# A hybrid decoder layer on one core: gate products in pairs of passes by width, and weight parts in pieces of 1024 columns

## The chip, the cores and the metric

The kernel runs on one core of one Trainium2 chip. The metric is the device time of one execution in microseconds (us), as the median of several runs. The engines of the core run side by side, each through its own queue in order: PE multiplies matrices (TensorE), ACT (ScalarE) and DVE (VectorE) do the elementwise work, POOL (GpSimd) a few additions, and SP (SyncE) issues the transfers from memory. They wait for each other on semaphores.

## The reference

One decoder layer, 256 tokens of 1024 features, in float32: a gated feed-forward network, three token mixers (A: sliding window attention, B: block attention, M: attention into 256 memory tokens) whose results are weighted by gates, and a second gated network, each followed by a layer norm.

```python
x = layer_norm(DN_ALPHA * x + 0.5 * swiglu(x, ffn1_w_gate, ffn1_w_up, ffn1_w_down), ln1_g, ln1_b)
h = x @ w_in + b_in
q_a, k_a, v_a, q_b, k_b, v_b, q_m, gates = jnp.split(h, offsets, axis=-1)
y_a = sliding_window_gqa(q_a, k_a, v_a, attn_sinks) @ w_proj_swa
y_b = moba_attention(q_b, k_b, v_b) @ w_proj_moba
y_m = memory_cross_attention(q_m, mem, w_mem_kv, b_mem_kv) @ w_proj_mem
g = jax.nn.sigmoid(gates.reshape(B, S, N_BRANCH, D))
mixed = (g[:, :, 0] * y_a + g[:, :, 1] * y_b + g[:, :, 2] * y_m) @ w_out
x = layer_norm(DN_ALPHA * x + mixed, ln2_g, ln2_b)
x = layer_norm(DN_ALPHA * x + 0.5 * swiglu(x, ffn2_w_gate, ffn2_w_up, ffn2_w_down), ln3_g, ln3_b)
```

## The kernel before

**Numbers in two parts.** Float32 values are held as a high and a low part, `hi` and `lo`, and a product is the sum of three: hi*hi, hi*lo and lo*hi. `split` (lines 129 to 132) makes the parts: ACT casts the source into `hi` (line 131), then DVE subtracts `hi` from the source and writes `lo` (line 132).

**Weights.** All weights come in chunks of 128x2048 elements, 1 MB each, in the order of `plan`. SP loads a chunk into one of three `raw` buffers (line 153), and `part_to` splits it into one of four pairs `whi`, `wlo`, so a `raw` is free for the next load once DVE has written its last `wlo`. `part_to` splits a chunk whole, 2048 columns at a time, or in four pieces of 512 columns (line 169): in pieces for the first six chunks, and for the 42 chunks from the last four of the first network's down projection to the gate and up weights of the second network's chunk 3, so for all that lies between the two networks' gate and up products. A chunk is prepared two chunks ahead of its use.

**Products.** One output tile is 128 features by 256 tokens in one of eight PSUM buffers `ps`. `feature_tile` (line 199) makes it with `product`: for each of 8 blocks of 128 inputs three matmuls of 256 columns, lines 187 to 189, 24 in all, summed in place. `feature_tile_2` (line 203) makes the same tile in two passes: 8 matmuls of 512 columns (line 209), in which `whi` meets high and low part of the tokens side by side, and 8 of 256 columns (line 211) for `wlo`. Its two halves have to be added: `added` (line 213) copies one half out with ACT (line 216) into `b`, and DVE adds the other half to it (line 217). The networks use `feature_tile_2`.

**The gates.** There are 24 gate tiles, named (c, b, j): column group c of 0 to 3, mixer b of 0 to 2, half j of 0 or 1. `gate_chunk` makes the two tiles of a (c, b). For c = 0 and 1 they stand among the attention's steps: `feature_tile`, then one ACT instruction, tanh with bias, from `ps` to `gates` (line 611). For c = 2 and 3 they stand among the mixing steps and already use `feature_tile_2`, `added`, and a tanh from `gates` to `gates` (lines 613 to 615).

**The attention.** `scores` (line 514) multiplies queries and keys (line 528, PE), on DVE adds the distance term (line 535, A and B) and takes row maxima (540, or 532 for M), negates them (543), lets ACT take the exponentials (551), and on DVE inverts the sums (560) and scales the probabilities (563). `turn` (line 566) transposes one pair of heads on PE (line 575) and splits the result into `p` (a 512 wide piece and, for A and B, a 256 wide one); `weigh` (line 582) multiplies `p` with the values `vab` (lines 187 to 189: two matmuls with the high part of `p`, one with the low part, on line 188) and splits the outcome into `qk_a` or `qk_b`. Lines 617 to 652 set the order in which all of this is written: `scores("b")`, gates (0, 1), `scores("m")`, gates (0, 2), `turn("b", 0)`, gates (1, 0), `weigh("b", 0)`, and so on.

**Who sets the order.** SP's queue stands as written. For PE, ACT and DVE a scheduler sets the order when the kernel is built, out of what is written and its own view of what is ready, so a change of sizes or of instructions shifts the others as well.

Of the kernel before, what the change touches and what calls it, by code (L numbers as in the profile page):

```python
# [13 lines left out]
AF = mybir.ActivationFunctionType  # L14
# [3 lines left out]
P = 128  # L18
S = 256
# [96 lines left out]
def hybrid_layer(ctx: ExitStack, tc: tile.TileContext, a: dict, out: bass.AP):  # L116
    nc = tc.nc
# [11 lines left out]
    def split(src, hi, lo):  # L129

        nc.scalar.copy(hi, src)  # L131
        return nc.vector.tensor_sub(lo, src, hi.bitcast(F32))  # L132
# [9 lines left out]
    index = {key: i for i, (key, _, _) in enumerate(chunks)}  # L142
# [4 lines left out]
    def load_to(n):  # L147
        while done["raw"] <= min(n, len(chunks) - 1):
            i = done["raw"]
            raw_of[i] = raws.tile([P, 2048], F32, name="raw")  # L150
            n_ = 512 if i < 4 else 2048
            for o in range(0, 2048, n_):
                nc.sync.dma_start(out=raw_of[i][:, o : o + n_], in_=a["w"][i][:, o : o + n_])
            done["raw"] += 1

    def part_to(n):
        while done["part"] <= min(n, len(chunks) - 1):
            i = done["part"]
            load_to(i)
            raw, how = raw_of.pop(i), chunks[i][1]  # L160
            if how:
                t = "1" if how == "leadg" else "2"
                hi = acts.tile([P, 2048], F32R, name="lhi", tag="A" + t)
                lo = acts.tile([P, 2048], F32R, name="llo", tag="B" + t)
            else:
                hi = parts.tile([P, 2048], F32R, name="whi")
                lo = parts.tile([P, 2048], F32R, name="wlo")

            n_ = 512 if i < 6 or index["mk"] - 4 <= i <= index["u", 2, 3] else 2048
            lows[i] = [split(raw[:, o : o + n_], hi[:, o : o + n_], lo[:, o : o + n_]) for o in range(0, 2048, n_)]  # L170
            part_of[i] = (hi, lo)
            done["part"] += 1

    def weights(key, ahead=2):
        i = index[key]
        load_to(i + 6)
        part_to(i + ahead)
        return part_of.pop(i)

    def prepare(key):  # L180
        part_to(index[key])

    def product(ps, terms, first=True, last=True):

        n = len(terms)
        for i, ((lh, ll), (rh, rl)) in enumerate(terms):
            nc.tensor.matmul(ps, lh, rh, start=first and i == 0, stop=False)  # L187
            nc.tensor.matmul(ps, lh, rl, start=False, stop=False)  # L188
            nc.tensor.matmul(ps, ll, rh, start=False, stop=last and i == n - 1)  # L189

    def two(t, *s):
        return tuple(x[s] for x in t)
# [6 lines left out]
    def feature_tile(ps, w, col, x, n=KD):  # L199

        product(ps, [(two(w, ALL, slice(k * 256 + col, k * 256 + col + P)), two(x, ALL, k, ALL)) for k in range(n)])

    def feature_tile_2(ps, w, col, x, ks=range(KD), parts_=(0, 1)):

        for part in parts_:
            for k in ks:
                wk = w[part][:, k * 256 + col : k * 256 + col + P]
                if part == 0:
                    nc.tensor.matmul(ps, wk, x.both[:, k], start=k == 0, stop=False)  # L209
                else:  # L210
                    nc.tensor.matmul(ps[:, S:], wk, x[0][:, k], start=False, stop=k == KD - 1)  # L211

    def added(dst, ps):

        b = work.tile([P, 512], F32, name="b", tag="w")[:, :S]
        nc.scalar.copy(b, ps[:, S:])  # L216
        nc.vector.tensor_add(dst, ps[:, :S], b)
# [23 lines left out]
    def tokens_of(name):  # L241

        both = acts.tile([P, KD, 2, S], F32R, name=name, tag="xT")
        return Parts(both)
# [39 lines left out]
    bcol = const.tile([P, NB], F32, name="bcol")  # L284
# [158 lines left out]
    x1T = tokens_of("x1T")  # L443
# [18 lines left out]
    for j in range(2):  # L462
        ps = mm.tile([P, 512], F32, name="ps")
# [4 lines left out]
    for t in range(2):  # L468
        ps = mm.tile([P, 512], F32, name="ps")
# [130 lines left out]
    gate_w = {}  # L600

    def gate_chunk(c, b, js=(0, 1)):
        if js[0] == 0:
            gate_w[c, b] = weights(("gt", c, b))
        for j in js:
            ps = mm.tile([P, 512], F32, name="ps")
            k = 12 + 8 * b + 2 * c + j
            g = gates[:, c % 2, 2 * b + j, :]
            if c < 2:
                feature_tile(ps[:, :S], gate_w[c, b], j * P, x1T)  # L610
                nc.scalar.activation(g, ps[:, :S], AF.Tanh, bias=bcol[:, k : k + 1], scale=0.5)  # L611
            else:
                feature_tile_2(ps, gate_w[c, b], j * P, x1T)
                added(g, ps)
                nc.scalar.activation(g, g, AF.Tanh, bias=bcol[:, k : k + 1], scale=0.5)

    tiles("qa0", [(0, qa, 0), (1, qa, 1)])
    tiles("qa1", [(2, qa, 2), (3, ka, 0)])
# [11 lines left out]
    weigh("a", 1)  # L630
    turn("a", 2)
    gate_chunk(0, 0)
    weigh("a", 2)
    scores("b")
    gate_chunk(0, 1)
    scores("m")
    gate_chunk(0, 2)
    turn("b", 0)
    gate_chunk(1, 0)
# [115 lines left out]
```

## Time and profile before

| | us |
|---|---|
| median of 3 runs (580.15 to 580.31) | 580.24 |
| the profiled execution | 580.73 |
| span of the profiled execution, first to last instruction | 578.9 |
| PE busy | 568.6 |
| DVE busy | 397.6 |
| ACT busy | 309.5 |
| POOL busy | 23.6 |

PE is shown busy in 98% of the span, but its matmuls overlap and the end of one is modelled, so for PE the distance from start to start is what counts. ACT and DVE are busy in 53% and 69% of the span, unevenly: in the attention, between 240 and 300 us, both are near full. A row of a timeline gives the start from the span's begin, the length, the engine, the line and what is written from what; "x4" merges four that follow each other, and a bracket names idle time of the engine before the row and what ended it.

### The profile page before, as it was taken

The numbers are of one execution on the slowest core, as the hardware profiler recorded it, in microseconds if no ns is written. First come the engines' busy times: TensorE is split into PE (matmuls) and PEld (weight loads), VectorE is DVE, ScalarE is ACT, GpSimd is POOL, SyncE is SP. The second block draws the span as 40 slices with busy tenths as digits, with TensorE's granted clock in tenths as the row PEclk, the third lists the DMA queues.
The fourth block names the chain that finished last, engine by engine and source line by source line (L and its number), as shares of the span: only waits on it lengthen the run. The fifth ranks groups of instructions, "written<-read, shape, count | busy, mean of one in ns | idle before, by whom it ended". The sixth has DMA issues, their size and how long they took to land.

```text
span 578.9 us, 8791 instructions
## 1 busy us (share of the span) xinstructions
PE 568.6 (98%) x3470; PEld 505.9 (87%) x3470; DVE 397.6 (69%) x609; ACT 309.5 (53%) x543; POOL 23.6 (4%) x37
## 2 busy tenths in 40 slices
PE   8999999999999999999999999999999999999994
PEld 7888888888888998999999989888888888888884
DVE  5887667764446977698787677996667657654336
ACT  6884556644333653964975665643565554633300
POOL 2000000000000000000002022210000000000001
PEclk9999999999999999999999999999999999999998
DMA  8887647745553474084163554536554555545201
GB/s 272 309 301 289 239 170 282 267 157 212 197 174 142 146 278 158 3 341 167 29 232 110 215 188 175 218 145 254 192 208 166 198 190 177 216 151 213 74 1 72
DMA packets 18025, 108.98 MB, mean 188 GB/s; under 512 B 2112, under 2 KB 2368, under 8 KB 5696
## 3 DMA queue, kind: packets, MB, share of 16 engines
q1 hardware_dynamic: 17984, 108.43, 52.0%
q8 instruction: 27, 0.44, 0.3%
q14 instruction: 14, 0.11, 0.1%
HBM read 107.37 MB, written 1.05 MB: 187 GB/s over the span
## 4 chain that ended last, share of the span: by engine, by line
PE 93%; ACT 3%; DVE 2%; DMA 1%; issue 0%; POOLq 0%; SPq 0%; DVEq 0%
PE ps L209 29%; PE ps L187 15%; PE ps L188 15%; PE ps L189 15%; PE ps L211 15%; ACT whi L131 1%; ACT sc_b L551 1%; DMA raw<-in_w_dram 1%; PE ps L575 1%; PE ps L255 1%; DVE sc_b L535 0%; DVE m L540 0%; PE ps L528 0%; ACT gates L611 0%; DVE r L419 0%
## 5 line engine op out<-in xcount | busy, mean ns | idle before, releaser
L132 DVE TENSOR_TENSOR wlo<-raw,whi 128x512 fp32r<-128x512 f32 (+2 forms) x234 | 233.8, 1030 | 127.0 <-ACT whi L131 122.6
L131 ACT CAST whi<-raw 128x512 fp32r<-128x512 f32 (+2 forms) x234 | 196.6, 882 | 121.7 <-PE ps L189 59.7
L209 PE MATMUL ps<-x0T,whi 128*128 128x512 f32 x352 | 89.5, 393 | 1.0 <-ACT whi L131 1.0
L209 PEld LDWEIGHTS ps<-x0T,whi 128*128 128x128 f32 x352 | 62.9, 189 | 12.3 <-ACT whi L131 1.4
L188 PE MATMUL ps<-wlo,hh 128*128 128x512 f32 (+1 forms) x198 | 72.5, 366 | 0.0
L187 PE MATMUL ps<-whi,hh 128*128 128x512 f32 (+1 forms) x198 | 72.5, 366 | 0.0
L189 PE MATMUL ps<-whi,hl 128*128 128x512 f32 (+1 forms) x198 | 72.3, 365 | 0.0
L209 PE MATMUL ps<-x2T,whi 128*128 128x512 f32 x288 | 72.2, 392 | 0.0
L209 PEld LDWEIGHTS ps<-x2T,whi 128*128 128x128 f32 x288 | 51.8, 189 | 9.3
L187 PE MATMUL ps<-x1T,whi 128*128 128x256 f32 x192 | 55.2, 287 | 0.3 <-ACT sc_m L551 0.3
L216 ACT COPY b<-ps 128x256 f32<-128x256 f32 x92 | 33.6, 368 | 39.6 <-PE ps L211 38.2
L188 PE MATMUL ps<-x1T,whi 128*128 128x256 f32 x192 | 54.3, 283 | 0.0
L189 PE MATMUL ps<-x1T,wlo 128*128 128x256 f32 x192 | 54.3, 283 | 0.0
L211 PEld LDWEIGHTS ps<-x0T,wlo 128*128 128x128 f32 x352 | 48.7, 190 | 4.2 <-DVE wlo L132 0.3
L211 PE MATMUL ps<-x0T,wlo 128*128 128x256 f32 x352 | 50.0, 282 | 0.0
L187 PEld LDWEIGHTS ps<-whi,hh 128*128 128x128 f32 x198 | 37.3, 188 | 6.1
L189 PEld LDWEIGHTS ps<-whi,hl 128*128 128x128 f32 x198 | 37.2, 188 | 6.2
L188 PEld LDWEIGHTS ps<-wlo,hh 128*128 128x128 f32 x198 | 37.3, 188 | 6.0
L211 PEld LDWEIGHTS ps<-x2T,wlo 128*128 128x128 f32 x288 | 39.3, 190 | 2.8
L211 PE MATMUL ps<-x2T,wlo 128*128 128x256 f32 x288 | 40.2, 282 | 0.0
L187 PEld LDWEIGHTS ps<-x1T,whi 128*128 128x128 f32 x192 | 36.8, 191 | 0.8 <-ACT sc_m L551 0.5
L188 PEld LDWEIGHTS ps<-x1T,whi 128*128 128x128 f32 x192 | 36.8, 192 | 0.0
(173 smaller groups left out, 762.8 us busy)
## 6 DMA issues: line engine op xcount, KB each, us to landing
raw<-in_w_dram SPq DMA_DIRECT2D x92, 1024.0 KB, 4.8
raw<-in_w_dram SPq DMA_DIRECT2D x16, 256.0 KB, 5.4
ln<-in_ln_dram SPq DMA_DIRECT2D x3, 1024.0 KB, 6.9
xT<-in_xT_dram SPq DMA_DIRECT2D x4, 256.0 KB, 6.5
x_sb<-in_x_dram SPq DMA_DIRECT2D x1, 1024.0 KB, 8.4
raw<-in_memT_dram SPq DMA_DIRECT2D x1, 1024.0 KB, 4.8
out_dram<-r SPq DMA_DIRECT2D x3, 256.0 KB, 2.1
brow<-in_by_column_dram SPq DMA_DIRECT2D x1, 387.0 KB, 8.5
```

The lines of the kernel that those rows point to most:

```text
L131: nc.scalar.copy(hi, src)
L132: return nc.vector.tensor_sub(lo, src, hi.bitcast(F32))
L187: nc.tensor.matmul(ps, lh, rh, start=first and i == 0, stop=False)
L188: nc.tensor.matmul(ps, lh, rl, start=False, stop=False)
L189: nc.tensor.matmul(ps, ll, rh, start=False, stop=last and i == n - 1)
L209: nc.tensor.matmul(ps, wk, x.both[:, k], start=k == 0, stop=False)
L211: nc.tensor.matmul(ps[:, S:], wk, x[0][:, k], start=False, stop=k == KD - 1)
L216: nc.scalar.copy(b, ps[:, S:])
L255: nc.tensor.transpose(ps[:, j * P : (j + 1) * P], src[:, k * P : (k + 1) * P], ident)
L551: nc.scalar.activation(sc[:, e, c0:c1], raw[e][:, c0:c1], AF.Exp, bias=negm[:, e, t : t + 1], scale=SCALE, accum_out=ssum[:, e, t : t + 1])
L575: nc.tensor.transpose(pt[:, s * n + j * P : s * n + (j + 1) * P], sc[:, 2 * i + s, c : c + P], ident)
```

## The change

For c = 0 and 1 the gate tiles are now made as those of c = 2 and 3 are: two passes of 16 matmuls instead of 24 matmuls, a copy on ACT, an addition on DVE, and the tanh from `gates` to `gates`. And where the weights' parts were made in pieces of 512 columns between the two networks' gate and up products, the pieces are now 1024 columns; the first six chunks keep theirs.

```diff
-            n_ = 512 if i < 6 or index["mk"] - 4 <= i <= index["u", 2, 3] else 2048
+            n_ = 512 if i < 6 else 1024 if index["mk"] - 4 <= i <= index["u", 2, 3] else 2048
...
-            if c < 2:
-                feature_tile(ps[:, :S], gate_w[c, b], j * P, x1T)
-                nc.scalar.activation(g, ps[:, :S], AF.Tanh, bias=bcol[:, k : k + 1], scale=0.5)
-            else:
-                feature_tile_2(ps, gate_w[c, b], j * P, x1T)
-                added(g, ps)
-                nc.scalar.activation(g, g, AF.Tanh, bias=bcol[:, k : k + 1], scale=0.5)
+            feature_tile_2(ps, gate_w[c, b], j * P, x1T)
+            added(g, ps)
+            nc.scalar.activation(g, g, AF.Tanh, bias=bcol[:, k : k + 1], scale=0.5)
```

With it the scheduler sets another order on ACT and DVE; on PE and SP the steps keep their places. Three places follow, first before, then after. Buffers carry a number that differs between the two programs.

ACT ahead of the exponentials of mixer B, from the last cast of `p` for A's second pair of heads: the two tiles of gates (0, 0), the result of A's third pair (`qk_a`), and the first tile of gates (0, 1). Before:

```order
L131 CAST p_2595<-ps_2592 128x256
L131 CAST qk_a_1949<-ps_2572 64x256
L131 CAST whi_2757<-raw_2331 128x512
L611 ACTIVATE gates_1951<-ps_2611,bcol_185 128x256
L131 CAST whi_2876<-raw_2413 128x512
L611 ACTIVATE gates_1951<-ps_2637,bcol_185 128x256
L131 CAST whi_2876<-raw_2413 128x512
L131 CAST qk_a_1949<-ps_2663 64x256
L131 CAST whi_2876<-raw_2413 128x512 x2
```

After:

```order
L131 CAST p_2531<-ps_2528 128x256
L216 COPY b_2560<-ps_2543 128x256
L611 ACTIVATE gates_1923<-gates_1923,bcol_185 128x256
L131 CAST whi_2784<-raw_2357 128x1024
L216 COPY b_2581<-ps_2564 128x256
L131 CAST whi_2784<-raw_2357 128x1024
L131 CAST qk_a_1921<-ps_2585 64x256
L611 ACTIVATE gates_1923<-gates_1923,bcol_185 128x256
L131 CAST qk_a_1921<-ps_2585 64x256
```

The tanh, which read `ps`, now reads what DVE's addition writes, and a cast of weights that stood apart from it stands behind it.

DVE at the same place, from the low part of that `p` to the first distance term of B. Before:

```order
L132 TENSOR_TENSOR p_2596<-ps_2592,p_2595 128x256
L132 TENSOR_TENSOR wlo_2758<-raw_2331,whi_2757 128x512 x2
L132 TENSOR_TENSOR wlo_2877<-raw_2413,whi_2876 128x512 x2
L132 TENSOR_TENSOR qk_a_1949<-ps_2663,qk_a_1949 64x256
L132 TENSOR_TENSOR wlo_2877<-raw_2413,whi_2876 128x512
L132 TENSOR_TENSOR qk_a_1949<-ps_2663,qk_a_1949 64x256
L535 SCALAR_TENSOR_TENSOR sc_b_2674<-dist_b_188,ps_2676 128x384
```

After:

```order
L132 TENSOR_TENSOR p_2532<-ps_2528,p_2531 128x256
L217 TENSOR_TENSOR gates_1923<-ps_2543,b_2560 128x256
L132 TENSOR_TENSOR wlo_2785<-raw_2357,whi_2784 128x1024
L217 TENSOR_TENSOR gates_1923<-ps_2564,b_2581 128x256
L132 TENSOR_TENSOR qk_a_1921<-ps_2585,qk_a_1921 64x256
L132 TENSOR_TENSOR wlo_2785<-raw_2357,whi_2784 128x1024
L132 TENSOR_TENSOR qk_a_1921<-ps_2585,qk_a_1921 64x256
L535 SCALAR_TENSOR_TENSOR sc_b_2596<-dist_b_188,ps_2598 128x384
```

The first addition stands behind the low part of `p`, and the `wlo` that follows it needs the `whi` that ACT casts behind the tanh of that addition.

DVE after the last scaling of M, from the low parts of `p` for B's first pair of heads to those of its second pair. Before:

```order
L132 TENSOR_TENSOR p<-ps,p 128x512
L132 TENSOR_TENSOR wlo<-raw,whi 128x512
L132 TENSOR_TENSOR p<-ps,p 128x256
L132 TENSOR_TENSOR wlo<-raw,whi 128x512 x5
L132 TENSOR_TENSOR qk_b<-ps,qk_b 64x256
```

After:

```order
L217 TENSOR_TENSOR gates<-ps,b 128x256 x2
L132 TENSOR_TENSOR p<-ps,p 128x512
L132 TENSOR_TENSOR wlo<-raw,whi 128x1024
L132 TENSOR_TENSOR p<-ps,p 128x256
L132 TENSOR_TENSOR wlo<-raw,whi 128x1024
L217 TENSOR_TENSOR gates<-ps,b 128x256
L132 TENSOR_TENSOR wlo<-raw,whi 128x1024
L217 TENSOR_TENSOR gates<-ps,b 128x256
L132 TENSOR_TENSOR wlo<-raw,whi 128x1024
L132 TENSOR_TENSOR qk_b<-ps,qk_b 64x256
```

Two additions stand ahead of the first `p`, and between the two pairs' `p` stand three pieces of 1024 and two additions instead of five pieces of 512; in both programs a `p` 128x512 follows the row of `qk_b`.

## Rows read from the trace of the kernel before

**Rows 1.** The chain of work that ended last, share of the span by engine.

```profile
PE 93%; ACT 3%; DVE 2%; DMA 1%; issue 0%; POOLq 0%; SPq 0%; DVEq 0%
```

**Rows 2.** Windows: stretch, its length, busy us and count of each engine, granted clock, DMA.

```profile
270.00:280.00 10.00, 9.70 (x90) 9.20 (x89) 6.99 (x20) 8.19 (x34) 0.00 (x0) 1.00 0.12 48
280.00:290.00 10.00, 10.00 (x82) 9.70 (x81) 9.24 (x23) 9.97 (x28) 0.00 (x0) 1.00 0.20 62
```

**Rows 3.** PE, timeline: first matmul of gates (0, 0), and the first of `weigh`.

```profile
255.78 0.36 PE L187 MATMUL ps<-x1T,whi 128*128 128x256 f32 x1
...
261.62 0.40 PE L187 MATMUL ps<-p,vab 128*128 128x512 f32 x1
```

**Rows 4.** The chain in order of time (start, length): one gate tile of c = 2.

```profile
312.46 1.84 PE ps L209 x8
314.30 0.95 PE ps L211 x8
```

**Rows 5.** Groups by line and shape: line, engine, count, busy us, mean ns, idle before.

```profile
L131 ACT CAST whi<-raw 128x512 fp32r<-128x512 f32 x182 | 103.5, 621 | 60.3 <-PE ps L189 29.9 <-DMA raw<-in_w_dram 12.2 <-PE ps L188 9.2
L131 ACT CAST whi<-raw 128x2048 fp32r<-128x2048 f32 x48 | 91.6, 1908 | 59.7 <-PE ps L189 29.8 <-PE ps L209 28.0 <-DMA raw<-in_w_dram 1.8
L216 ACT COPY b<-ps 128x256 f32<-128x256 f32 x92 | 33.6, 368 | 39.6 <-PE ps L211 38.2 <-issue 1.3
L615 ACT ACTIVATE gates<-gates,bcol 128x256 f32<-128x256 f32 x12 | 6.1, 509 | 4.3 <-DVE gates L217 4.3
L132 DVE TENSOR_TENSOR wlo<-raw,whi 128x512 fp32r<-128x512 f32 x182 | 122.2, 711 | 38.6 <-ACT whi L131 34.2 <-PE ps L211 4.0
L132 DVE TENSOR_TENSOR wlo<-raw,whi 128x2048 fp32r<-128x2048 f32 x48 | 110.1, 2293 | 86.6 <-ACT whi L131 86.6
L217 DVE TENSOR_TENSOR gates<-ps,b 128x256 f32<-128x256 f32 x12 | 5.0, 420 | 0.8 <-ACT b L216 0.6
```

**Rows 6.** DVE, timeline from A's `p` to B's scaling.

```profile
245.57 1.05 DVE L132 TENSOR_TENSOR p<-ps,p 128x512 fp32r<-128x512 f32 x2
...
260.20 0.42 DVE L132 TENSOR_TENSOR p<-ps,p 128x256 fp32r<-128x256 f32 x1
...
262.40 0.69 DVE L132 TENSOR_TENSOR wlo<-raw,whi 128x512 fp32r<-128x512 f32 x1 [0.57 <-ACT whi L131]
...
265.44 1.02 DVE L535 SCALAR_TENSOR_TENSOR sc_b<-dist_b,ps 128x384 f32<-128x384 f32 x2
...
277.48 2.84 DVE L563 TENSOR_SCALAR sc_b<-sc_b,rs 128x128 f32<-128x128 f32 x12
280.24 1.29 DVE L132 TENSOR_TENSOR wlo<-raw,whi 128x512 fp32r<-128x512 f32 x2
```

**Rows 7.** ACT, timeline: weights' casts ahead of M's exponentials, and the first of these.

```profile
277.45 1.13 ACT L131 CAST whi<-raw 128x512 fp32r<-128x512 f32 x2
278.48 0.47 ACT L551 ACTIVATE sc_m<-ps,negm 128x256 f32<-128x256 f32 x1
```

**Rows 8.** DVE, timeline: `p` of B's first and second pair of heads.

```profile
285.79 0.42 DVE L132 TENSOR_TENSOR p<-ps,p 128x256 fp32r<-128x256 f32 x1
...
289.47 0.67 DVE L132 TENSOR_TENSOR p<-ps,p 128x512 fp32r<-128x512 f32 x1
```

**Rows 9.** PE, timeline: the steps that take what DVE and ACT give.

```profile
247.52 0.28 PE L188 MATMUL ps<-p,vab 128*128 128x256 f32 x1
...
278.43 0.82 PE L575 MATMUL ps<-ident,sc_b 128*128 128x128 f32 x6
279.55 0.38 PE L187 MATMUL ps<-x1T,whi 128*128 128x256 f32 x1 [0.30 <-ACT sc_m L551]
...
286.27 0.38 PE L188 MATMUL ps<-p,vab 128*128 128x256 f32 x1
...
290.36 0.40 PE L188 MATMUL ps<-p,vab 128*128 128x512 f32 x1
...
291.19 0.39 PE L188 MATMUL ps<-p,vab 128*128 128x256 f32 x1
```

## The prediction

> **What bounds the kernel now.** I read the chain of waits first: 93% of what ended last is PE [rows 1], so the time is the sum of PE's start-to-start distances, and an edit counts only by what it does to that sum. Then the windows, to see where PE can be made to wait: in the attention DVE and ACT, idle a third to a half of the whole span, are busy 7 to 10 of 10 us [rows 2]. Then the timelines of the three engines there. In this stretch PE takes its operands almost the moment they are made. The transposes of B's probabilities start at 278.43, when the third of twelve scalings, begun at 277.48 and 0.24 apart, is just done [rows 6, 9]; the fourth, which the fourth transpose needs, leaves about 0.2. The matmul with B's first low part of `p` starts at 286.27, 0.06 after DVE's write of it that begins at 285.79 and lasts 0.42 [rows 8, 9]; that of the second pair at 290.36, after a write that ends at 290.14. One wait shows: 0.30 ahead of gates (1, 0), for a PSUM buffer that M's exponentials hold [rows 9]. The granted clock is full here (1.00) [rows 2]. So this stretch has next to no slack, and the change adds work to DVE and ACT in it.
>
> **What PE saves.** Two gate tiles by `feature_tile` stand from 255.78 to 261.62, 5.84 us [rows 3]. By two passes a tile is 1.84 + 0.95 = 2.79 [rows 4], two are 5.58, and with 0.1 for the slow first matmul after transposes (255.78 shows 0.36 in place of 0.28) 5.68. That is 0.16 for a pair, 0.08 a tile, and for the 12 tiles 0.95 us. No other PE instruction changes. This term is safe: from 0.9 to 1.1.
>
> **What ACT and DVE pay.** Each of the 12 tiles gains a copy on ACT (0.37) and an addition on DVE (0.42), and its tanh is one of 0.51 [rows 5]. Two that follow each other on an engine overlap by some 0.08 on DVE and 0.1 on ACT: two `wlo` of 512 take 1.29, not 1.42, two `whi` 1.13, not 1.24 [rows 6, 7, 5]. So the step is 0.33 for an addition and 0.27 for a copy, 4.0 us on DVE and 3.2 on ACT in sum. A piece of 1024 is read off between 512 and 2048: DVE 711 + (2293 - 711)/3 = 1240 ns, ACT 621 + (1908 - 621)/3 = 1050 ns [rows 5], against 1.29 and 1.13 for two of 512; so DVE wins about 0.06 and ACT about 0.08 for each of 84 pairs, 5 and 7 us over a third of the program. Where the engine waits anyway, outside the attention, neither sum touches PE. In the attention what counts is who stands in front of whom.
>
> [...] The rows give 0.06 a pair once the overlap counts.
>
> **Place 1, about 247.** The order now puts a `wlo` of 1024 between the two low parts of `p` for A's first pair, which ran back to back from 245.57 and ended at 246.62 [rows 6]. PE wants the second at 247.52 [rows 9], 0.9 later. The piece moves it to 246.62 + 1.14 = 247.76, less 0.1 that the pieces before it save: a wait of about 0.2, with 0.1 for the longer cast on ACT 0.3. Ends: 0 and 0.7.
>
> **Place 2, the transposes of B at 278.43.** Before the first distance term three things grow on DVE. Ahead of the `p` at 260.20 stand pieces of 1024 where one of 512 stood, half a piece more, +0.5. Then comes the hand-over: addition (0.42), the tanh on ACT that reads it (0.51), the cast of `whi` behind that tanh (1.05), and only then the next `wlo`. DVE, done with the addition after 0.33, stands for about 1.6. In the old order it had casts in hand: from 260.20 to 265.44 are 5.24 us with 4.0 of steps (0.34, five pieces at 0.60, two halves of `qk_a` at 0.33), so 1.2 of idle, 0.57 of it in one row [rows 6]. The new steps sum to the same 4.0 (0.34 + 2 x 0.33 + 2 x 1.14 + 2 x 0.33), with 1.6 of idle and some 0.15 for `qk_a`: +0.5. Behind the first distance term, a `wlo` of 0.6 goes, an addition of 0.33 comes, and a tanh stands before the first exponential with 0.3: 0. So the scalings come 1.0 later, and PE arrives six tiles x 0.08 = 0.5 sooner, less the 0.2 of slack: a wait of 1.25. Ends: 0.6, if the idle that was there covers most of it, and 2.0, if none does. ACT, blocked at the tanh, holds the casts queued behind it, and DVE and PE wait for those.
>
> **Place 3, gates (1, 0) at 279.55.** Two casts of `whi` (1.13) that stood ahead of M's exponentials [rows 7] are gone, so these follow 1.1 sooner after B's, and the buffer is free earlier; the transposes go at the pace of the scalings meanwhile. The wait of 0.30 becomes 0.2: -0.1. Ends: -0.3 and +0.1.
>
> **Place 4, `weigh("b", 0)` at 286.27.** Counted from the first scaling of B (277.48): M's exponentials start 1.1 earlier, which moves M's scalings 1.1 forward; two additions (0.67) and a larger piece (+0.5) come ahead of the second low part of `p`. So it ends at +8.8, as before (285.79 + 0.42 - 277.48 = 8.73). PE, held by the fourth scaling (done at +1.0) and not by the old wait, does three transposes (0.35), waits 0.2 to 0.3, makes two tiles in 5.7 and is at this matmul after 0.87 more: +8.3. Wait 0.5; ends 0.2 and 0.7. Here the shorter tiles are given back.
>
> **Place 5, `weigh("b", 1)` at 290.36.** From the second `p` of the first pair to the first `p` of the second, DVE needs 289.47 - 285.79 = 3.68 [rows 8]; five pieces of 0.60 become three of 1.14 and two additions of 0.33, +1.07. PE needs 290.36 - 286.27 = 4.09 for its part [rows 9], now 4.01. After place 4 PE has no slack to this chain: from the end of one write to the end of the other are 3.68 + 1.07 + 0.67 - 0.42 = 5.0, so PE waits 1.0. The second half, at 291.19, has ACT's tanh and a cast of 0.95 in front of its chain: +0.15. In sum 1.15; ends 0.7 and 1.5.
>
> **The rest.** Later gate tiles stand between transposes with fewer rows in front of them; the mixing steps and the norms have pieces of weights only, prepared two chunks ahead: 0.1, ends 0 and 0.5. SP's queue keeps its order, and a `raw` comes free with the last `wlo` of its chunk, within 1 us of where it did; ACT's idle for loads shows a few such waits off PE's path.
>
> **Sum.** -0.95 + 0.3 + 1.25 - 0.1 + 0.5 + 1.15 + 0.1 = +2.25 us, on the profiled execution's 580.73 (span 578.9 and 1.8 around it). That execution lies 0.49 above the median of the runs, 580.24, so the median becomes 582.5.
>
> **Rivals.**
> *Relief.* Larger pieces empty ACT and DVE faster than the gates fill them (5 and 7 us against 4.0 and 3.2), the wait of 0.30 goes, and no new one comes: 580.24 - 0.95 - 0.30 = 579.0. For it speaks the sum over the stretch; against it the order at places 2 and 5, where the additions stand ahead of what PE waits for. [...] Chance 0.05.
> *Half hidden.* Place 2 costs its lower end, because DVE's idle takes the hand-over, and place 1 nothing, while 4 and 5 cost 0.2 and 0.9: -0.95 + 0.6 - 0.1 + 0.2 + 0.9 = +0.65, 580.9. For it: 1.2 us of idle in the old order at just that place. Chance 0.13.
> *Buffers.* A `ps` of a gate was free after one ACT instruction; now it is held until DVE's addition, and that of gates (0, 1) stands behind twelve scalings. If the next users of these eight buffers are PE's next transposes, PE waits for whole rows of DVE at two more places, 0.9 each: +4.0, 584.3. For it: the wait of 0.30, which is of this kind. Against: in the built program these transposes wait, beside the scalings, for ACT alone. It decides from an addition that ends later than the last tile before its buffer's reuse. Chance 0.12.
>
> **How the numbers follow.** The forecast, 582.5, has 0.70. A measurement of this kernel can tell about 0.2% (1.16 us) from no change, so under 579.1 is faster and over 581.4 slower. The forecast's own range, from the ends above taken half way, is 581.5 to 583.6. Half hidden lies within 0.2%, relief just on the faster side, buffers above. So: faster 0.05, same 0.13, slower 0.82. The range from 581.0 to 584.2 takes in the forecast, the upper part of half hidden and most of buffers.
>
> **What would show it.** In the changed profile: gate tiles of 1.84 and 0.95 from 255 on; DVE idle of over 1 us before a `wlo` near 262, put down to ACT; transposes of `sc_b` that start apart from each other after a wait of over 1 us; waits ahead of line 188 of 0.5 near 286 and 1.0 near 291; nothing new outside 245 to 312. I am wrong if PE runs through place 2 and place 5 without a wait, or if the new waits are for buffers.

## The result

The changed kernel takes 583.82 us (median of 4 runs, 583.39 to 584.54) against 580.25 (580.15 to 580.31): a ratio of 1.0063, with a 95% interval from 1.0045 to 1.0080. It is slower, by 3.6 us. A second set of five runs gave 583.49 (583.04 to 583.73) against 580.45: 1.0049, 1.0036 to 1.0062.

The page of the changed kernel, busy times and instruction counts, and the chain that ended last by engine:

```profile
PE 570.9 (98%) x3374; PEld 503.0 (86%) x3374; DVE 393.1 (67%) x537; ACT 305.5 (52%) x471; POOL 25.2 (4%) x37
...
PE 86%; DVE 5%; ACT 5%; issue 1%; DMA 1%; POOLq 0%; SPq 0%; DVEq 0%; ACTq 0%
```

DVE is busy for 4.5 us less than before and ACT for 4.0 less (397.6 and 309.5 were their sums), and still the program is longer: PE's part of the chain fell from 93% to 86%, and DVE and ACT took most of what it lost, 5% each after 2% and 3% [rows 1]. The groups by shape, line, engine, count, busy us and mean ns, idle before:

```profile
L132 DVE TENSOR_TENSOR wlo<-raw,whi 128x1024 fp32r<-128x1024 f32 x80 | 98.2, 1247 | 42.1 <-ACT whi L131 42.1
L131 ACT CAST whi<-raw 128x1024 fp32r<-128x1024 f32 x80 | 81.2, 1052 | 55.7 <-PE ps L189 30.9 <-DMA raw<-in_w_dram 6.9 <-issue 5.2
...
L611 ACT ACTIVATE gates<-gates,bcol 128x256 f32<-128x256 f32 x24 | 11.8, 514 | 16.3 <-DVE gates L217 16.2
```

A piece of 1024 costs 1247 and 1052 ns, read off beforehand as 1240 and 1050 between the two sizes of [rows 5]. What grew is the tanh's wait for DVE's addition: 16.2 us in sum over 24 tiles, after 4.3 over the 12 that had one before [rows 5].

**Where PE waits now.** First the profile of the second set (x5_again below), whose granted clock is 1.00 in every window from 240 to 320. Its first matmul of the memory keys and its first of the mixing step, then the same two of the kernel before:

```profile
190.62 0.28 PE L187 MATMUL ps<-memT,whi 128*128 128x256 f32 x1
...
309.32 0.28 PE L187 MATMUL ps<-qk_a,whi 128*128 128x256 f32 x1
```

```profile
190.63 0.28 PE L187 MATMUL ps<-memT,whi 128*128 128x256 f32 x1
...
306.39 0.28 PE L187 MATMUL ps<-qk_a,whi 128*128 128x256 f32 x1
```

Between these two steps, from here on "the stretch", PE needs 118.70 us instead of 115.76: +2.94. Behind it, up to the last matmul, both kernels take 264.4. So the whole difference lies where the forecast put it. PE in that profile, by rows (start, length, a bracket for what it waited for):

```profile
247.40 0.28 PE L187 MATMUL ps<-p,vab 128*128 128x256 f32 x1
247.90 0.39 PE L188 MATMUL ps<-p,vab 128*128 128x256 f32 x1 [0.23 <-DVE p L132]
...
277.51 1.11 PE L211 MATMUL ps<-x1T,wlo 128*128 128x256 f32 x8
279.61 1.18 PE L575 MATMUL ps<-ident,sc_b 128*128 128x128 f32 x6 [0.99 <-DVE sc_b L563]
281.01 2.12 PE L209 MATMUL ps<-x1T,whi 128*128 128x512 f32 x8 [0.22 <-ACT sc_m L551]
...
286.71 0.40 PE L187 MATMUL ps<-p,vab 128*128 128x512 f32 x1
...
287.41 0.28 PE L187 MATMUL ps<-p,vab 128*128 128x256 f32 x1
288.02 0.39 PE L188 MATMUL ps<-p,vab 128*128 128x256 f32 x1 [0.33 <-DVE p L132]
...
291.81 0.40 PE L187 MATMUL ps<-p,vab 128*128 128x512 f32 x1
293.01 0.50 PE L188 MATMUL ps<-p,vab 128*128 128x512 f32 x1 [0.80 <-DVE p L132]
293.35 0.40 PE L189 MATMUL ps<-p,vab 128*128 128x512 f32 x1
293.85 0.38 PE L187 MATMUL ps<-p,vab 128*128 128x256 f32 x1
294.37 0.39 PE L188 MATMUL ps<-p,vab 128*128 128x256 f32 x1
```

A bracket counts from the modelled end of the matmul before, so a wait is better read as the distance from start to start, less what that matmul takes where nothing is late (in this profile 0.23 with 512 columns, 246.70 to 246.93, and 0.12 with 256, 262.67 to 262.79; 0.11 from one transpose to the next, 255.21 to 255.32 in the kernel before; for the last transpose ahead of place 3 an estimate of 0.06, half of what 256 columns take). The five places are those that the prediction numbers. So read, place 1 costs 247.90 - 247.40 - 0.12 = 0.39 (0.38 from the rounded rows), place 2 1.15 ahead of the transposes (the pass before ends 0.95 after 277.51) and 0.34 between them, place 3 0.43 in place of 0.51 before, place 4 0.49, place 5 0.97 and 0.67. The first matmul behind a wait takes some 0.1 more as well (247.90 to the next at 248.13 is 0.23 and not 0.12); these tenths are not counted in the places.

**The first profile has one thing more.** Its stretch took 118.99. PE at place 2 and after it, and then the windows (stretch, length, busy us and count of PE, PEld, DVE, ACT and POOL, granted clock, DMA):

```profile
266.19 2.09 PE L209 MATMUL ps<-x1T,whi 128*128 128x512 f32 x8 [0.19 <-DVE gates L217]
...
280.49 1.18 PE L575 MATMUL ps<-ident,sc_b 128*128 128x128 f32 x6 [1.07 <-DVE sc_b L563]
281.89 3.32 PE L209 MATMUL ps<-x1T,whi 128*128 128x512 f32 x8 [0.22 <-ACT sc_m L551]
286.34 2.00 PE L209 MATMUL ps<-x1T,whi 128*128 128x512 f32 x8
...
289.83 0.28 PE L187 MATMUL ps<-p,vab 128*128 128x256 f32 x1
289.94 0.28 PE L188 MATMUL ps<-p,vab 128*128 128x256 f32 x1
```

```profile
280.00:282.00 2.00, 1.29 (x7) 0.84 (x8) 1.96 (x10) 2.00 (x10) 0.00 (x0) 1.00 0.00 0
282.50:285.80 3.30, 3.30 (x11) 2.71 (x10) 2.82 (x12) 3.30 (x11) 0.00 (x0) 0.50 0.02 5
```

Behind place 2 the granted clock was 0.50, and the tile at 281.89 took 286.34 - 281.89 = 4.45 in place of 2.91 in the other profile (281.01 to 283.92): 1.54 lost. In exchange place 4 shows no wait (289.94 follows 289.83 by 0.11) and place 5 only 0.67: PE came late enough for the low parts. The row at 266.19 holds one more wait, 0.34 by the distance of starts, for a PSUM buffer that DVE's addition for gates (0, 0) holds. So a slow clock that took 1.54, with that wait, made the stretch longer by no more than 0.29.

### The profile page after: what moved, and what is told of

Its sections match the earlier page's. It is cut to its first block, busy times and chain, and to the rows that moved or that the text cites. A ratio compares the mean times of both kernels' runs of the same rounds, so it can differ in the third digit from the quotient of the medians.

```text
span 582.8 us, 8463 instructions
## 1 busy us (share of the span) xinstructions
PE 570.9 (98%) x3374; PEld 503.0 (86%) x3374; DVE 393.1 (67%) x537; ACT 305.5 (52%) x471; POOL 25.2 (4%) x37
## 4 chain that ended last, share of the span: by engine, by line
PE 86%; DVE 5%; ACT 5%; issue 1%; DMA 1%; POOLq 0%; SPq 0%; DVEq 0%; ACTq 0%
PE ps L209 31%; PE ps L211 16%; PE ps L188 13%; PE ps L187 13%; PE ps L189 13%; DVE wlo L132 1%; ACT whi L131 1%; DMA raw<-in_w_dram 1%; DVE m L540 1%; ACT sc_a L551 1%; ACT sc_b L551 1%; PE ps L575 1%; ACT sc_m L551 1%; PE ps L255 1%; DVE sc_b L535 0%
## 5 line engine op out<-in xcount | busy, mean ns | idle before, releaser
L132 DVE TENSOR_TENSOR wlo<-raw,whi 128x1024 fp32r<-128x1024 f32 (+3 forms) x154 | 224.2, 1471 | 132.7 <-ACT whi L131 132.7
L131 ACT CAST whi<-raw 128x1024 fp32r<-128x1024 f32 (+3 forms) x154 | 187.4, 1240 | 119.8 <-PE ps L189 60.7
L216 ACT COPY b<-ps 128x256 f32<-128x256 f32 x104 | 37.8, 368 | 43.0 <-PE ps L211 41.4
L209 PE MATMUL ps<-x1T,whi 128*128 128x512 f32 x192 | 50.0, 403 | 0.4 <-ACT sc_m L551 0.2
L209 PEld LDWEIGHTS ps<-x1T,whi 128*128 128x128 f32 x192 | 35.1, 192 | 7.4 <-ACT sc_m L551 0.5
L211 PEld LDWEIGHTS ps<-x1T,wlo 128*128 128x128 f32 x192 | 26.7, 194 | 2.0
L187 PE MATMUL ps<-x1T,whi 128*128 128x256 f32 x96 | 27.3, 285 | 0.0
L189 PE MATMUL ps<-x1T,wlo 128*128 128x256 f32 x96 | 27.2, 283 | 0.0
```

## The experiments

All times are medians beside runs of the kernel before on the same chip (580.35, 580.45 and 580.45 in three sets); the ratio is to those. "Stretch" is as above, from each run's profile, and 115.76 before.

| run | what differs | us | ratio (95%) | stretch |
|---|---|---|---|---|
| x5_again | the changed kernel | 583.49 | 1.0049 (1.0036 to 1.0062) | 118.70 |
| x1_gates | gates alone | 583.28 | 1.0054 (1.0041 to 1.0066) | 119.95 |
| x2_pieces | pieces alone | 582.28 | 1.0030 (1.0018 to 1.0042) | 117.26 |
| x3_tanh_late | changed, tanh of (0, 0) later | 582.81 | 1.0041 (1.0028 to 1.0053) | 117.18 |
| x4_second_column | changed, c = 0 as before | 582.15 | 1.0030 (1.0018 to 1.0041) | 117.66 |
| x6_warm | changed, zeros at place 2 | 583.76 | 1.0056 (1.0043 to 1.0070) | 119.22 |
| x7_last_gates | before, (1, 1) and (1, 2) | 580.54 | 0.9996 (0.9988 to 1.0005) | 115.83 |
| x8_gate10 | before, (1, 0) | 582.39 | 1.0035 (1.0022 to 1.0049) | 117.45 |
| x9_gate00 | before, (0, 0) | 581.50 | 1.0019 (1.0010 to 1.0028) | 116.95 |
| x10_gate00_late | the same, tanh later | 580.85 | 1.0006 (0.9996 to 1.0016) | 116.22 |

**x1_gates: the gates without the pieces.**

```diff
-            n_ = 512 if i < 6 else 1024 if index["mk"] - 4 <= i <= index["u", 2, 3] else 2048
+            n_ = 512 if i < 6 or index["mk"] - 4 <= i <= index["u", 2, 3] else 2048
```

> All gates in two passes, the parts of the weights in pieces of 512 as before the change. Forecast's account: PE saves its 0.95 us; place 1 (a longer piece ahead of A's second low part, 0.39 in the changed kernel's trace) is gone; place 2 keeps the hand-over ACT copy, DVE addition, ACT tanh and so a wait of 1.0 to 1.8 at the transposes near 279; place 5 keeps two additions in front of the low parts, 1.0 to 1.8. Sum about +2.5: 582.2 to 583.3. Rival, the pieces do the harm: without the large pieces the additions find room, 579.3 to 580.3. Second rival, the fall of the granted clock costs over 1 us by itself once PE waits 1 us at place 2: 583.5 to 584.5.

Measured 583.28, the upper end of the first account and 0.2 under the second rival's range. PE's rows at place 5:

```profile
292.31 0.50 PE L187 MATMUL ps<-p,vab 128*128 128x512 f32 x1 [1.15 <-ACT p L131]
293.21 0.71 PE L188 MATMUL ps<-p,vab 128*128 128x512 f32 x1 [0.40 <-DVE p L132]
```

Places 1 and 4 are gone, places 2 and 5 cost 2.0 each, both above the 1.0 to 1.8 expected: at place 5 the wait is for the high part of `p` from ACT too. Within place 5 the clock fell to 0.50, from about 293.3 to 296.7, although it had stayed at 1.00 behind place 2. One window of it (as above):

```profile
294.00:295.00 1.00, 1.00 (x6) 0.91 (x6) 1.00 (x3) 0.36 (x2) 0.00 (x0) 0.50 0.00 0
```

From line 188 at 293.21 on, the rest of `weigh`, six transposes and the next tile take 1.6 more than the same steps at the full clock, and no later wait is shorter for it, so here the slow clock adds to the stretch in full. This profiled execution took 584.73, 1.45 above the median of its run, so the 119.95 in the table is not that of the median. By the medians the gates' part loses 2.9 by itself, the whole change 3.0 to 3.6: that the pieces alone do the harm is refuted.

**x2_pieces: the pieces without the gates**, the opposite edit on the kernel before.

> The kernel before with the pieces of 1024 alone; gates as before. Forecast's account: places 1 and 4, where a larger piece stands ahead of a low part of p, cost 0.3 to 0.4 and 0.5 to 0.6, place 5 some 0.15, place 2 nothing: 580.9 to 581.5, with the granted clock full. Rival, larger pieces only empty DVE and ACT sooner and cost nothing in front of PE: 579.9 to 580.3. Rival, pieces make place 2 as well: 581.5 to 582.5, and the granted clock falls near 282.

Measured 582.28, above the first account's range by 0.8 and within that of the rival that I had tied to place 2, but without its mechanism: the transposes follow without a wait and the clock is full (1.00 in every window from 240 to 320). PE's rows at place 4, and at a place that the forecast did not have, the first pair of M:

```profile
286.82 0.28 PE L187 MATMUL ps<-p,vab 128*128 128x256 f32 x1
287.51 0.38 PE L188 MATMUL ps<-p,vab 128*128 128x256 f32 x1 [0.42 <-DVE p L132]
...
301.71 0.50 PE L188 MATMUL ps<-p,vm 128*128 128x512 f32 x1 [0.18 <-DVE p L132]
```

Place 1 costs 0.40, place 4 0.58, M's pair 0.34, place 5 0.29 (0.24 before), 1.37 more than before in sum; the stretch is longer by 1.50. So larger pieces lose alone, although DVE's busy time is 389.2, 8.4 us less than before. The two halves of the change lose 2.9 and 1.9 alone and 3.0 to 3.6 together: they aren't additive, since with the additions in the queue places 2 and 5 cost less with the larger pieces (1.49 and 1.64) than with pieces of 512 (2.0 and 2.0). That it is so because fewer DVE and ACT steps stand in the queues is likely, but no run shows it by itself.

**x3_tanh_late: the hand-over taken apart.** The work is the same; only ACT's order changes.

```diff
-    scores("b")
+    queue_behind(scores("b"), [tanh[k] for k in (12, 13) if k in tanh])
```

(`scores` here returns its last exponential, and `tanh` holds the gates' tanh by column.)

> The changed kernel; the two tanh of gates (0, 0) are queued on ACT behind the exponentials of B, so that ACT does not stand at a tanh that waits for DVE's addition while a cast of whi is behind it. No work is added or left out. Forecast's account (the hand-over is a part of place 2): DVE's wait of 1.5 us near 262 shrinks below 0.7, the wait ahead of the transposes near 279 falls from 1.56 by 0.5 to 1.0; the wait moves in part to place 3 and 4; 582.0 to 583.0 against 583.8. Rival (DVE's and ACT's sum of work sets place 2, whoever stands first): no change, 583.4 to 584.2. If the granted clock falls because PE stands over 1 us at place 2, it stays full here, and 581.8 to 582.5 follow.

Measured 582.81, within the first account's range. DVE at the hand-over, first in the changed kernel (x5_again), then here, where the two `wlo` follow the addition of 262.14 at once:

```profile
260.83 1.02 DVE L132 TENSOR_TENSOR p<-ps,p 128x512 fp32r<-128x512 f32 x2
261.77 0.41 DVE L217 TENSOR_TENSOR gates<-ps,b 128x256 f32<-128x256 f32 x1
263.70 1.23 DVE L132 TENSOR_TENSOR wlo<-raw,whi 128x1024 fp32r<-128x1024 f32 x1 [1.51 <-ACT whi L131]
...
267.22 2.87 DVE L535 SCALAR_TENSOR_TENSOR sc_b<-dist_b,ps 128x384 f32<-128x384 f32 x6
...
279.18 2.84 DVE L563 TENSOR_SCALAR sc_b<-sc_b,rs 128x128 f32<-128x128 f32 x12
```

```profile
262.51 2.36 DVE L132 TENSOR_TENSOR wlo<-raw,whi 128x1024 fp32r<-128x1024 f32 x2
...
265.46 0.53 DVE L535 SCALAR_TENSOR_TENSOR sc_b<-dist_b,ps 128x384 f32<-128x384 f32 x1
...
277.98 2.84 DVE L563 TENSOR_SCALAR sc_b<-sc_b,rs 128x128 f32<-128x128 f32 x12
```

DVE's 1.51 us of standing is gone, the first distance term comes 1.8 sooner and the scalings 1.2, and PE starts the transposes without a wait. A new wait of 0.60 appears among them, place 3 grows from 0.43 to 0.68, both for PSUM that M's exponentials hold, since the two tanh now stand in front of these, and place 4 costs 0.78. The stretch is 1.5 shorter, the median 0.7 to 1.0; in the profile 0.8 of it is lost behind PE's last matmul (8.7 from its end to the span's end in place of 7.9), while the output is written.

**x4_second_column: gates of c = 0 as before.**

```diff
-            feature_tile_2(ps, gate_w[c, b], j * P, x1T)
-            added(g, ps)
-            nc.scalar.activation(g, g, AF.Tanh, bias=bcol[:, k : k + 1], scale=0.5)
+            if c == 0:
+                feature_tile(ps[:, :S], gate_w[c, b], j * P, x1T)
+                nc.scalar.activation(g, ps[:, :S], AF.Tanh, bias=bcol[:, k : k + 1], scale=0.5)
+            else:
+                feature_tile_2(ps, gate_w[c, b], j * P, x1T)
+                added(g, ps)
+                nc.scalar.activation(g, g, AF.Tanh, bias=bcol[:, k : k + 1], scale=0.5)
```

> The changed kernel with gates (0, 0) to (0, 2) in three products a tile as before, gates (1, 0) to (1, 2) in two passes, pieces of 1024. Forecast's account: PE loses 0.48 of its gain; place 2 (transposes near 279) is gone with its 1.5 us, and the clock stays full; place 4, hidden in the changed kernel's trace by PE's slow tiles, opens at 0.5 to 0.8; place 5 stays at 1.0 to 1.3: 582.0 to 582.8. Rival (place 2 comes from the larger pieces): it stays above 0.8 and the time is 583.5 to 584.5. Rival (with place 2 gone nothing is late any more): 580.0 to 581.0.

Measured 582.15, as the first account has it. PE:

```profile
285.69 0.28 PE L187 MATMUL ps<-p,vab 128*128 128x256 f32 x1
286.55 0.38 PE L188 MATMUL ps<-p,vab 128*128 128x256 f32 x1 [0.58 <-DVE p L132]
...
290.91 0.49 PE L187 MATMUL ps<-p,vab 128*128 128x512 f32 x1 [0.38 <-ACT p L131]
291.64 0.50 PE L188 MATMUL ps<-p,vab 128*128 128x512 f32 x1 [0.23 <-DVE p L132]
```

Place 2 is gone with the tiles that made it, in spite of the larger pieces; place 4 costs 0.74, and place 5 1.04 and 0.23. The clock is full (1.00 in every window from 240 to 320).

**x5_again: the changed kernel once more.**

> The changed kernel once more. In its first profile the granted clock fell near 282 (0.74 over 280 to 285), which made 14 matmuls 1.6 us longer and hid place 4. If this fall belongs to the kernel, the profile shows it again, place 4 without a wait and place 5 at 0.7, and the time is 583.4 to 584.5. If it comes in some executions only, this profile has the full clock, place 4 opens at 0.5 to 0.8, place 5 at 1.0 to 1.4, and the time is 583.0 to 584.0 all the same, since the slow tiles only took the place of these waits. The wait of 0.34 for a PSUM buffer near 266 should be there in both cases.

The clock was full (1.00 from 240 to 320) and places 4 and 5 opened, to 0.49 and 1.64; the time was 583.49. The fall of the clock came in one of the two profiled executions, and here it doesn't set the time (a stretch of 118.99 with it, 118.70 without): of the 1.54 that it took, the waits behind it gave back all but 0.29 (in x1_gates it stood behind the last long wait, and nothing gave it back). But the wait of 0.34 near 266 in the first profile, for a PSUM buffer that DVE's addition for gates (0, 0) holds, isn't there: this one, too, came in one of the two.

**x6_warm: zeros in the wait.**

```diff
             pt = acc.tile([P, 512], F32, name="ps")
+            if (nm, i, cs) == ("b", 0, (0, 128)):
+                for _ in range(20):
+                    nc.tensor.matmul(pt[:, :P], idle, idle, start=True, stop=True)
```

> The changed kernel with 20 matmuls of zeros (bfloat16, 128 x 128, no wait) by PE into the transposes' own PSUM tile just ahead of place 2; they fill the wait of 1.2 us, and their result is overwritten. If the clock falls because PE stands there, it stays at 1.00 over 280 to 300; place 4 then waits 0.5 to 0.8 and place 5 1.0 to 1.4, and the time is 583.0 to 584.0: the fall had cost nothing beyond what these waits cost. If the fall adds to the sum, the time is 581.8 to 582.6. If it has another cause than the wait, it is there again near 282 and the time stays at 583.4 to 584.5. The 20 matmuls may stand 0 to 0.3 past the wait's end.

Inconclusive on the clock: it was full (1.00 from 240 to 320), but so it was in x5_again without the zeros. At 583.76 nothing is gained, and the profile says why: the added matmuls also made the scheduler put one more piece in front of `p`. DVE behind the two additions that follow M's scalings:

```profile
286.21 1.22 DVE L132 TENSOR_TENSOR wlo<-raw,whi 128x1024 fp32r<-128x1024 f32 x1
287.35 0.69 DVE L132 TENSOR_TENSOR p<-ps,p 128x512 fp32r<-128x512 f32 x1
```

In the changed kernel no `wlo` stands between the additions and this `p`. Place 4 cost 0.75 and 0.78 here: one piece more in front, one microsecond more of waiting. The buffer wait near 266 was back, with 0.47.

**x7_last_gates: two passes where PE doesn't wait close behind.** The kernel before, with the condition `c == 0 or (c, b) == (1, 0)` for three products in place of `c < 2`.

> The kernel before, with two passes for gates (1, 1) and (1, 2) alone, four tiles, pieces of 512. Forecast's account: an addition does no harm where no low part of p or scaling that PE waits for stands close behind it; (1, 2) stands among M's transposes, (1, 1) behind place 5. PE saves 4 x 0.08 = 0.32 and no new wait comes: 579.8 to 580.3. Rival: every gate tile between transposes delays the next low part: 580.8 to 581.5.

Measured 580.54 against 580.45, 0.9996 (0.9988 to 1.0005): no loss, and no gain that a measurement can tell, 0.2 above the first account's range and under the rival's. The stretch is 115.83 in place of 115.76: the 0.32 saved went into 0.16 at M's first pair, 0.05 at place 5 and smaller ones.

**x8_gate10 and x9_gate00: one chunk alone.** The kernel before, with two passes for gates (1, 0), or for gates (0, 0), and nothing else.

> The kernel before with two passes for gates (1, 0) alone, two tiles, pieces of 512. These two tiles stand right ahead of weigh b0 and b1. Forecast's account: PE saves 0.16; two additions of DVE and two tanh on ACT come between the p of the first pair and that of the second, so place 5 opens by 1.0 to 1.9 and nothing else changes: 581.2 to 582.2, a loss of ten times what is saved. Rival: a chunk alone finds room, as gates (1, 1) and (1, 2) did, 580.1 to 580.6.

> The kernel before with two passes for gates (0, 0) alone, two tiles, pieces of 512. Forecast's account: the hand-over DVE addition, ACT tanh, ACT cast, DVE low part costs DVE some 0.7 to 1.2 ahead of B's distance terms, PE comes 0.16 sooner, 0.2 of slack: a wait of 0.6 to 1.1 at the transposes and some 0.1 more at place 3: 580.9 to 581.8. Rival: DVE's idle of 1.2 us in that place takes it: 580.1 to 580.6.

Measured 582.39, 0.2 above the first account's range, and 581.50, within it. Two tiles of (1, 0) save PE 0.16, and the program is 1.9 longer; PE's rows:

```profile
291.19 0.50 PE L187 MATMUL ps<-p,vab 128*128 128x512 f32 x1 [0.93 <-ACT p L131]
291.92 0.50 PE L188 MATMUL ps<-p,vab 128*128 128x512 f32 x1 [0.22 <-DVE p L132]
```

Places 1 to 4 are as before but for 0.21 at place 4 (0.05 before), and all the rest is place 5: 1.09, 0.50 and 0.22. Here the first wait is for ACT's cast of `p`, so ACT is what is late, not DVE's low part. Between its casts of `p` for the two pairs (284.80 and 290.57, before 284.82 and 288.67) stand not only two copies more, but seven casts of weights instead of five: the scheduler moved two of them there. How much of the 1.9 is theirs no run shows.

**x10_gate00_late: x9 with the tanh later**, by the edit of x3_tanh_late.

> The same as the run with gates (0, 0) alone, but with their two tanh queued on ACT behind the exponentials of B. Forecast's account: DVE has no idle before a low part near 262, the scalings start 0.5 to 1.1 sooner than in that run, and the transposes do not wait; the time falls by 0.4 to 0.9 against it, to 580.3 to 581.1. Rival (the additions themselves fill DVE): the same time as without the later tanh, within 0.2.

DVE's first `wlo` behind the first addition, in x9_gate00, then in this run, with its pieces between the low parts of B's first two pairs:

```profile
263.11 0.69 DVE L132 TENSOR_TENSOR wlo<-raw,whi 128x512 fp32r<-128x512 f32 x1 [1.09 <-ACT whi L131]
```

```profile
261.54 0.68 DVE L132 TENSOR_TENSOR wlo<-raw,whi 128x512 fp32r<-128x512 f32 x1
...
285.00 4.30 DVE L132 TENSOR_TENSOR wlo<-raw,whi 128x512 fp32r<-128x512 f32 x7
```

The idle time is gone, and the transposes' wait with it (0.85 in x9_gate00, none here); 580.85 against 581.50, and ten of the twelve times lie below all twelve of x9_gate00. The additions are the same, and near 262 only who stands behind whom differs. What is left of the loss, 0.4 with an interval that takes in none, shows at place 5 (0.27 and 0.77): between the two pairs' low parts DVE now has seven pieces of weights, in x9_gate00 and in the kernel before five. No version was faster than the kernel before.

## Why the prediction was right, point by point

The forecast was 582.5 in a range of 581.0 to 584.2, slower with 0.82. The time was 583.8 and 583.5 in two sets. By its terms, against the profile with the full clock (x5_again):

| term | forecast | measured |
|---|---|---|
| PE saves | -0.95 | -0.95, the 12 tiles from start to start (gates (1, 0): 5.70, by forecast 5.68) |
| place 1 | +0.3 | +0.39 |
| place 2 | +1.25 | +1.49 |
| place 3 | -0.1 | -0.08 |
| place 4 | +0.5 | +0.44 (0.49 less 0.05 before) |
| place 5 | +1.15 | +1.40 (1.64 less 0.24 before) |
| rest | +0.1 | +0.25, left over from the stretch: mostly 0.1 each at places 1 and 5 for the first matmul behind a wait |
| sum | +2.25 | +2.94 |

- **What bounds it** held: nothing changed outside the attention, and the new waits stand at the places named, but for the one near 266 in the first profile. That the sums of DVE and ACT fall while PE waits more is the case in one line.
- **Place 2** was right in its mechanism, which x3_tanh_late, x4_second_column, x9_gate00 and x10_gate00_late show: the addition itself is cheap (0.41 long in x5_again), and the tanh behind it, which keeps ACT from the cast that DVE needs next, is not (ACT stands 1.86 at it there). DVE's idle row was forecast as 1.6 and is 1.51. That 1.25 came so near 1.49 is in part luck, for two sizes were off and nearly cancel. The first is "half a piece more, +0.5". The low part that began at 260.20 before [rows 6] is the second of the row `p` x2 at 260.83, whose own 0.42 ends the row at 261.85, so it begins near 261.43: 1.23 later. Place 1 isn't the reason, since the cast of `whi` with which ACT's work for it starts waits for its load, and starts as early as before (first before, then x5_again):

```profile
256.28 0.62 ACT L131 CAST whi<-raw 128x512 fp32r<-128x512 f32 x1 [2.43 <-DMA raw<-in_w_dram]
```

```profile
256.19 1.05 ACT L131 CAST whi<-raw 128x1024 fp32r<-128x1024 f32 x1 [2.46 <-DMA raw<-in_w_dram]
```

DVE stands 0.46 for that longer cast, and from there on it works without a pause up to this low part, with two pieces of 1024 ahead of it. With the hand-over behind it, B's scalings come 279.18 - 277.48 = 1.70 later and not 1.0. The second is PE's arrival, put at "six tiles x 0.08 = 0.5 sooner": it is there at 277.51 + 0.95 = 278.46, before at 278.43, since place 1, with the matmul behind it 0.49, took back what six shorter tiles had saved. The prediction's sum has place 1 as a term of its own and left it out here.
- **Place 3** held: 0.43 in place of 0.51, a small gain.
- **Place 4** held, and x4_second_column (0.74) and x2_pieces (0.58) show it without place 2. Of its two causes, the additions and a larger piece, the piece is what counted: x1_gates, with the same two additions ahead and pieces of 512, waits 0.06 there.
- **Place 5**: from the second low part of the first pair to the first of the second pair the forecast had 3.68 + 1.07 = 4.75. DVE's rows:

```profile
287.55 0.41 DVE L132 TENSOR_TENSOR p<-ps,p 128x256 fp32r<-128x256 f32 x1
...
292.29 0.67 DVE L132 TENSOR_TENSOR p<-ps,p 128x512 fp32r<-128x512 f32 x1
293.43 0.43 DVE L132 TENSOR_TENSOR qk_b<-ps,qk_b 64x256 fp32r<-64x256 f32 x1 [0.47 <-ACT qk_b L131]
```

292.29 - 287.55 = 4.74, and the wait of 0.97 is the 1.0 forecast. What failed is the second half, put at +0.15: it costs 0.67 against 0.24, +0.43. ACT's tanh and a cast of 1024 stand in front of its casts of `qk_b` and `p`, and DVE stands 0.47 for them; I had counted the longer rows and not that they make ACT the late one.

- **Pieces.** The price of a piece was right (1247 and 1052 ns), its relief too small: x2_pieces shows DVE at 389.2 and ACT at 301.6, so 8.4 and 7.9 us less for 84 pairs, 0.10 and 0.09 a pair, where the forecast had 0.06 and 0.08. None of it reached PE: the larger pieces shortened the two engines' sums and not the program's time (582.28 against 580.35).
- **Rivals.** Relief and half hidden are out. Buffers, given 0.12 at two places of the transposes, did happen, but at one place, the tile of gates (0, 1) near 266, in two of the three profiles with this order there (0.34, x6_warm 0.47, and none in x5_again, where the addition ends 0.10 before PE starts the tile).
- **Not foreseen** was the fall of the clock; by the two profiles of the changed kernel it hardly moved the stretch (118.99 and 118.70).

## What to carry to other kernels

On a path that is fed just in time, an instruction isn't priced by its length: find what stands behind it in its engine's queue, and who needs that; two tiles that saved PE 0.16 us made the program 1.9 longer because of it. A step that goes from one engine to a second and back to the first held both queues here (in x5_again ACT stood 1.86 us at the tanh and DVE 1.51 at the next `wlo`), and moving its last part behind the urgent work, with no work left out, took the idle time away (x9 to x10: 1.09 us to none), though part of the gain went into later waits. Larger pieces relieved the sums of two engines by 8 us each, and the program was 1.9 longer (x2_pieces): where the next engine takes a result at once, look at the grain and not only at the sum. And since any edit lets the scheduler move pieces of weights about, read the new order before a difference is put down to the edit alone.

## What the runs showed that was not expected

- Between 240 and 320 us the granted clock fell to 0.50 in two profiles of twelve (1.00 in the other ten), each time behind waits of PE: in the changed kernel's first profile from about 282.5 to 285.8, behind place 2, and with the gates alone from about 293.3 to 296.7, in place 5. In the second, waits that were longer in sum at place 2 (1.64 and some 0.3 among the transposes) left it at 1.00. What tells the two apart is open; x6_warm could not show it.
- A wait and a slow clock need not add: in the changed kernel 1.54 us lost to the clock showed as 0.29 in the stretch, since PE then came to places 4 and 5 when their operands were ready. In x1_gates no such wait followed, and the 1.6 lost stayed in the stretch.
- The order that the scheduler sets reacts to far edits: twenty matmuls on PE moved a piece of 1.2 us in front of `p` on DVE, at a price of about 1 us (place 4 went from 0.49 to 1.53), and x8_gate10 and x10_gate00_late each moved two pieces of weights to a place where PE waits.
